# A hybrid attention and ConvFFN step on one core: a margin in the planner's TensorE list, a sample's loads traced later, and the sample's value product split by head

## The chip, the cores and the metric

One Trainium2 chip, one of its cores. The metric is the device time of one execution in microseconds (us); the median of several runs is compared. One further execution was recorded by the hardware profiler, and everything that is read below is read from that recording.

## The reference

One layer of a streaming encoder, run for a prompt of 1024 frames and a sample of 64 frames that share the weights, all in float32. The part that matters here:

```python
p = rms_norm(x, g_norm1) @ w_in            # q, k, v of 8 heads "A", 8 heads "B", forget logits
oa = softmax(qa ka^T / 8 + rel_bias) va    # A: band of 9 chunks of 64 frames
ob = softmax(qb kb^T / 8 + c_t - c_s) vb   # B: causal, c = running sum of log sigmoid(forget logits)
x += concat(oa, ob) @ w_o
x += mem_attend(rms_norm(x), mk, mv)       # 256 memory tokens; mk, mv = rms_norm(mem) @ w_mkv
x += conv_ffn(rms_norm(x))
```

The sample does the same with caches in front of its own keys and values: each of its 64 queries sees 512 cached rows (A) or 1024 cached rows (B) and then the sample's own 64. For each head the last step of its attention is a product of probabilities (64 queries by 576 or 1088 keys) with values (those keys by 64).

## The kernel before

TensorE products of float32 are made from two parts of each operand (`hi`, a float32r copy, and `lo`, the rest) in three products (`hi*hi`, `lo*hi`, `hi*lo`); only the sample's attention and a few small products use plain float32 operands.

The work goes in stages, heads in pairs. For each pair of heads the projection of eight blocks of 128 frames (L413, and L535 for the sample) is woven with the attention of blocks that are already projected: transposes of the normalised queries and keys (L484), a copy of the keys to the other half of the partitions by a DMA (L491, `k<-k`), scores (L706, into the one PSUM tile `S`), a reduction on VectorE that adds the bias and finds the extreme (L709, `mx`), the exponential on ScalarE (L711), the scaling on GpSimd (L713), transposes of the probabilities (L743, `PT<-ident,s`), their split into `pth` and `ptl` (L744 on ScalarE, L745 on VectorE), and the values (L762, `O`).

After the last pair comes the stage that most of the change touches. Its background work is the memory's keys and values, `mem @ w_mkv` (L829, `pj<-mw..`, in units of 128 by 256; `w_mkv` arrives by L813 as `mwraw` and is split by ScalarE at L821 and VectorE at L822). A finished unit of keys is scaled by VectorE (L958, `kv`) and turned by TensorE (L977). Into this the eight head pairs of the sample are woven, one `Sample` object for each in the order `SAMPLES`: `load` (L996 to L1005: queries, new values, cached keys and values), `load_bias` (L1014, L1016), `prep` (L1022), `score` (L1045 and L1046 on TensorE, L1048 and L1050 on VectorE, L1056 on ScalarE), `turn` (transposes L1069, copies to `pth` or `ptl` at L1071 and L1073), `sum` (the values, L1083) and `out` (L1093, L1095). A `sum` product takes the probabilities of both heads (128 columns, 64 for each head) as the stationary operand and the values of both heads (128 columns) as the moving one; of its 128 by 128 result only the two diagonal 64 by 64 blocks are used. There are 48 such products with 128 keys and 8 with the last 64 (`svn`). The output projection (L1183) follows, and its inputs are split at L1235 and L1236.

In the loop over the samples, step `x` weaves sample `x`'s scores, sample `x-1`'s turns and sums and sample `x+1`'s preparation with units of the background work. At the head of the step it loads the bias of sample `x+1` and the data of sample `x+3`.

What is traced up to the line that sets `arranged` (1627) is not executed in the order in which it was traced. `arrange` is a planner: it gives each instruction a cost, follows when each operand would be ready, and at every moment lets the engine that is free first take, of the instructions that are ready, the one that was traced earliest. The order that results is fixed on each engine (TensorE, VectorE, ScalarE, GpSimd, and the DMA queue of SyncE). All of it is in-order: an instruction whose operand is late holds up everything behind it on its engine. What is traced later than `arranged` keeps its traced order.

Of the kernel before, what the change touches and what calls it, by code (L numbers as in the profile page):

```python
# [9 lines left out]
ACT = mybir.ActivationFunctionType  # L10
# [7 lines left out]
S = 64  # L18
# [23 lines left out]
def hybrid_step(ctx: ExitStack, tc: tile.TileContext, i: dict, o: dict):  # L42
    nc = tc.nc
    act, dve, pool, pe = nc.scalar, nc.vector, nc.gpsimd, nc.tensor
# [343 lines left out]
    def weave(main, subs):  # L388
        j = 0
        for x, f in enumerate(main):  # L390
            f()
            while j * len(main) < len(subs) * (x + 1):
                subs[j]()
                j += 1
        for f in subs[j:]:
            f()
# [539 lines left out]
    kvs, stores, waiting = {}, [], []  # L936
# [45 lines left out]
    class Sample:  # L982
# [93 lines left out]
        def sum(self, c):  # L1076
            last = c == self.nc
            if c == 0:
                self.op = ps.tile([P, 2, P], F32, name="O", bufs=1)[:, 0]
            rows_, n = (S, 1) if last else (P, 4)  # L1080
            v = self.vraw.rearrange("p (o h) d -> p o h d", o=1) if last else self.v[c]
            for x in range(n):
                pe.matmul(self.op, self.pt[c][:rows_, x], v[:rows_, x].rearrange("p h d -> p (h d)"),  # L1083
                          start=c == 0 and x == 0, stop=last)
            if last:
                self.u = wk.tile([P, 64], F32, name="su", bufs=2)
                for h in range(2):
                    r = slice(h * S, h * S + S)
                    act.activation(self.u[r], self.op[r, h * S:h * S + S], ACT.Copy, scale=self.r[r])

        def out(self):
            tq = bank("PT").rearrange("p (a b) -> p a b", a=4)
# [37 lines left out]
    samples = [Sample(p) for p in SAMPLES]  # L1130
# [134 lines left out]
    for x in range(len(samples) + 1):  # L1265
# [4 lines left out]
        nxt = samples[x + 1] if x + 1 < len(samples) else None  # L1270
        if nxt:
            nxt.load_bias()
        if x + 3 < len(samples):
            samples[x + 3].load()
        if x in (5, 6):
            load_early(x - 5)
        new, fin = [], []
# [12 lines left out]
        elif ha:  # L1290
            main = pieces[4:] + [f for two in zip(split[1], first[1].pieces) for f in two]
            subs = [lambda: stream.upto(4)] + subs
        weave(main, subs)
        if cur:
            c = cur.nc
            old = [lambda z=z, u=cur: u.turn(z) for z in range(2)] + [lambda u=cur: u.sum(0)]
            old += ([lambda u=cur: u.turn(2), lambda u=cur: u.sum(1)] if c == 2 else [])
            old += [lambda u=cur, c=c: u.sum(c), cur.out]
# [243 lines left out]
    for n, u in enumerate(mems):  # L1542
        h, c = u.h, u.c
# [69 lines left out]
    for w, m in enumerate(ROWS):  # L1613
        x = long_row("qhi")
# [472 lines left out]
def arrange(tc, end):  # L2087

    import heapq

    signal = 0.07
    nodes, owner, made, touched, opened, closed = [], {}, {}, {}, {}, []
    writer, readers, group = {}, {}, {}
    setter = select = None
# [19 lines left out]
    def cost(ins, engine, kind, cols, rows, psum):  # L2114

        op = str(getattr(ins, "op", ""))
        if engine == "PE":
            if getattr(ins, "is_transpose", False):
                return 0.109, 0.35, False
            if ins.ins[0].bass_ap.dtype == F32:  # L2120
                o = max(0.214, cols * 0.00178)
            else:
                o = max(0.00087 * ins.ins[1].bass_ap.ap[1][1], 0.003 + cols * 0.000456)
            return o, o + 0.16, False
# [131 lines left out]
    while True:  # L2256
        start, engine = min((earliest(e), e) for e in ENGINES)
        if start == 1e9:
            break
        while coming[engine] and coming[engine][0][0] <= start:  # L2260
            n = heapq.heappop(coming[engine])[1]
            heapq.heappush(waiting[engine][nodes[n][6]], n)
        a, b = waiting[engine]
        line = min([x for x in (a, b if port <= start else []) if x], default=None)
        if line is None:
            continue
# [18 lines left out]
                    release(m)  # L2285
        for m, begun in after[n]:
            same = nodes[m][1] == engine
            ready[m] = max(ready[m], start + (0 if begun else busy if same and engine == "PE" else done if same and engine != "SP" else done + signal))
            missing[m] -= 1
            if not missing[m]:  # L2290
                release(m)
# [91 lines left out]
```

## Time and profile before

| | |
|---|---|
| time, median of 3 runs | 1693.71 us (1690.34, 1693.71, 1694.01) |
| the profiled execution, its own time | 1686.39 us |
| its span | 1684.6 us |
| TensorE busy | 1660.5 us, 99% of the span |
| VectorE, ScalarE, GpSimd busy | 1166.4, 907.9, 583.2 us |
| DMA, mean of the core's 16 DMA engines | 119 GB/s |

The span is the time from the first to the last recorded instruction; the execution's own time is 1.8 us more than that. The profiled execution is 7.3 us under the median of the three runs. TensorE (PE) records have modelled ends: a product counts as busy for some 0.2 to 0.4 us though the next one begins after about 0.12, so a wait shorter than that overlap does not appear as idle time of PE. It appears in the start times and in the waits of the weight loads (PEld).

### The profile page before, as it was taken

What the parts mean: (1) busy time and instruction counts of PE and PEld (TensorE: products, weight loads), DVE (VectorE), ACT (ScalarE), POOL (GpSimd) and SP (SyncE); (2) the same over time, 40 slices, a digit from 0 to 9 for tenths busy, and PEclk for the clock granted to TensorE, in tenths of its full rate; (3) what the DMA queues carried; (4) which work ended last, traced back from release to release, by engine and by line L of the source; (5) the groups of instructions that cost most, each with busy time, mean ns of one, the idle gap of its engine ahead of it and who ended that gap; (6) DMA issues with size and microseconds to landing.
All of it is one profiled execution on the core that took longest, in us unless ns stands there. A gap on an engine that the chain in (4) does not pass through costs nothing.

```text
span 1684.6 us, 33070 instructions
## 1 busy us (share of the span) xinstructions
PE 1660.5 (99%) x12027; PEld 1613.2 (96%) x12027; DVE 1166.4 (69%) x2584; ACT 907.9 (54%) x2003; POOL 583.2 (35%) x846
## 2 busy tenths in 40 slices
PE   9999999999999999999999999999999999999999
PEld 8899899999998879999999999999999999999999
DVE  7866866766778644344553797777777777559996
ACT  8866677767777564345555554333333333444442
POOL 1756688888853213444446111000000000000000
PEclk9999999999999999999999999999999999999999
DMA  7323243232235974421115632222222222983332
GB/s 242 91 77 84 76 113 91 77 92 84 64 118 165 290 216 152 141 82 58 55 58 162 214 115 84 77 78 77 78 77 77 78 78 84 320 298 120 102 109 88
DMA packets 142260, 199.82 MB, mean 119 GB/s; under 512 B 22200, under 2 KB 85304, under 8 KB 142096
## 3 DMA queue, kind: packets, MB, share of 16 engines
q1 hardware_dynamic: 142096, 197.70, 37.8%
q8 instruction: 95, 1.56, 0.4%
q14 instruction: 69, 0.57, 0.1%
HBM read 148.01 MB, written 43.34 MB: 114 GB/s over the span
## 4 chain that ended last, share of the span: by engine, by line
PE 87%; ACT 4%; DVE 4%; DMA 2%; issue 1%; SPq 0%; POOL 0%; DVEq 0%; ACTq 0%; POOLq 0%
PE W L1739 27%; PE W L2063 14%; PE pj L1183 14%; PE pj L413 11%; PE S L706 4%; PE O L762 3%; PE PT L743 3%; PE pj L829 2%; PE W L1183 1%; PE pj L535 1%; PE S L1475 1%; PE tq L1514 1%; PE O L1514 1%; PE tq L484 1%; DMA k<-k 1%
## 5 line engine op out<-in xcount | busy, mean ns | idle before, releaser
L413 PE MATMUL pj<-whi,xhi 128*128 128x384 f32 (+1 forms) x480 | 172.7, 360 | 0.0
L413 PE MATMUL pj<-whi,xlo 128*128 128x384 f32 (+1 forms) x480 | 164.7, 343 | 0.0
L413 PE MATMUL pj<-wlo,xhi 128*128 128x384 f32 (+1 forms) x480 | 164.1, 342 | 0.0
L1739 PE MATMUL W<-h,hi 128*128 128x272 f32 x704 | 134.3, 288 | 1.4 <-ACT qlo L1875 1.4
L1845 POOL COPY s<-gp 128x2 f32<-128x2 f32 x22 | 15.8, 719 | 336.1 <-DVE gp L1844 336.1
L2063 PE MATMUL W<-f,hi 128*128 128x272 f32 x672 | 127.2, 287 | 0.0
L745 DVE TENSOR_TENSOR ptl<-PT,pth 128x512 fp32r<-128x512 f32 (+2 forms) x192 | 97.9, 521 | 32.4 <-ACT pth L744 30.6
L713 POOL TENSOR_SCALAR s<-s,ssum 128x640 f32<-128x640 f32 (+7 forms) x128 | 92.9, 728 | 68.2 <-DVE ssum L712 52.2
L711 ACT ACTIVATE s<-s,mx 128x640 f32<-128x640 f32 (+7 forms) x128 | 94.5, 738 | 35.9 <-DVE mx L709 35.0
L744 ACT CAST pth<-PT 128x512 fp32r<-128x512 f32 (+2 forms) x192 | 84.6, 451 | 54.1 <-PE PT L743 52.4
L1739 PEld LDWEIGHTS W<-h,hi 128*128 128x128 f32 x704 | 110.3, 188 | 1.7 <-ACT qlo L1875 1.6
L2063 PEld LDWEIGHTS W<-f,hi 128*128 128x128 f32 x672 | 105.2, 188 | 0.1
L1739 PE MATMUL W<-h,lo 128*128 128x272 f32 x352 | 101.3, 288 | 0.0
L706 PE MATMUL S<-k,q 128*128 128x256 f32 (+3 forms) x432 | 90.5, 323 | 7.2 <-DVE mx L709 2.8
L2063 PE MATMUL W<-f,lo 128*128 128x272 f32 x336 | 96.7, 288 | 0.0
L1602 ACT CAST hi<-raw 128x512 fp32r<-128x512 f32 x68 | 42.2, 621 | 98.7 <-PE W L1739 59.2
L413 PEld LDWEIGHTS pj<-whi,xhi 128*128 128x128 f32 x480 | 90.6, 189 | 1.5
L413 PEld LDWEIGHTS pj<-wlo,xhi 128*128 128x128 f32 x480 | 90.8, 189 | 0.7
L413 PEld LDWEIGHTS pj<-whi,xlo 128*128 128x128 f32 x480 | 90.3, 188 | 0.4
L743 PE MATMUL PT<-ident,s 128*128 128x128 f32 x528 | 87.6, 273 | 0.8 <-DVE ptl L745 0.8
L706 PEld LDWEIGHTS S<-k,q 128*128 128x128 f32 x432 | 67.3, 188 | 21.8 <-DVE q L495 8.1
L1183 PE MATMUL pj<-a,hi 128*128 128x384 f32 (+1 forms) x352 | 87.2, 332 | 1.0 <-DVE a L1236 0.9
(611 smaller groups left out, 5684.3 us busy)
## 6 DMA issues: line engine op xcount, KB each, us to landing
raw<-in_w_down_dram SPq DMA_DIRECT2D x45, 256.0 KB, 2.7
wraw<-in_w_dram SPq DMA_DIRECT2D x56, 192.0 KB, 2.7
raw<-in_w_up_dram SPq DMA_DIRECT2D x41, 256.0 KB, 2.7
h<-ad SPq DMA_DIRECT2D x32, 272.0 KB, 5.1
mwraw<-in_w_mkv_dram SPq DMA_DIRECT2D x16, 512.0 KB, 5.6
raw<-in_w_mo_dram SPq DMA_DIRECT2D x32, 256.0 KB, 3.2
kvraw<-in_w_down_dram SPq DMA_DIRECT2D x32, 256.0 KB, 3.4
k<-k SPq DMA_DIRECT2D x60, 128.0 KB, 2.4
```

The costliest lines, as they stand in the source:

```text
L413: pe.matmul(pj[:, :nw], x_part(a, k, t * P, P), wt[k][b][:, :nw], start=n == 0, stop=n == 3 * KT - 1)
L706: pe.matmul(sp[:, a:a + m], q, ring[:, h, z, k0:k0 + m], start=z == 0, stop=z == 1)
L711: act.activation(s[:, :n], s[:, :n], ACT.Exp, bias=mx, scale=-1.0, accum_out=sm)
L713: pool.tensor_scalar(s[:, :n], s[:, :n], sm, 1.0, op0=ALU.mult, op1=ALU.mult)
L743: pe.transpose(pt[:, b - ch[0]], self.s[j][:, (b - w0) * P:(b - w0 + 1) * P], ident)
L744: act.copy(hi[:, f:f + n, j], pt[:, f:f + n])
L745: dve.tensor_tensor(lo[:, f:f + n, j], pt[:, f:f + n], f32(hi[:, f:f + n, j]), op=ALU.subtract)
L762: pe.matmul(op[:r, cols], v[:, :r], self.pts[b][m][:, x, cols], start=first and (b, m) == steps[0], stop=ch[-1] == self.last and (b, m) == ...
L1183: pe.matmul(out()[:, :cn], w[a][:, k % 4], x[b][k][:, c0:c0 + cn], start=k == 0 and (a, b) == SPLIT[0], stop=k == KT - 1 and (a, b) == SPL ...
L1602: act.copy(hi, t)
L1739: pe.matmul(w[:, z, :Q], a(p, j), rights[j][b][:, z * Q:z * Q + Q], start=fresh and begin and j == 0 and x == 0, stop=final and end and j ...
L2063: pe.matmul(ws[m][:, z, :Q], la[p][:, m * P:(m + 1) * P], ra[b][:, z * Q:z * Q + Q], start=first and y == 0 and what in opening, stop=fina ...
```

## The change

Four edits.

1. `sum` makes two products for each group of keys, one for each head: 64 columns of probabilities as the stationary operand, 64 columns of values as the moving one, into the partitions of that head. The two blocks that nobody used are not computed. The scaled copy to `su` becomes one instruction on 128 partitions in place of two on 64.
2. The planner's cost of a float32 product whose stationary operand has at most 64 columns is 0.077 us (it was at least 0.214).
3. `samples[x + 3].load()` is traced after the step's weave and not at its head, so that in the planner the step's other loads go before it.
4. A margin for TensorE, `sure["PE"] = 0.2`: while TensorE has anything else that is ready, an instruction joins its list only when its operands have been ready for 0.2 us by the planner's reckoning. Successors on TensorE itself are exempted by the same 0.2.

```diff
             for x in range(n):
-                pe.matmul(self.op, self.pt[c][:rows_, x], v[:rows_, x].rearrange("p h d -> p (h d)"),
-                          start=c == 0 and x == 0, stop=last)
+                for h in range(2):
+                    r = slice(h * S, h * S + S)
+                    pe.matmul(self.op[r, :64], self.pt[c][:rows_, x, r], v[:rows_, x, h], start=c == 0 and x == 0, stop=last)
             if last:
                 self.u = wk.tile([P, 64], F32, name="su", bufs=2)
-                for h in range(2):
-                    r = slice(h * S, h * S + S)
-                    act.activation(self.u[r], self.op[r, h * S:h * S + S], ACT.Copy, scale=self.r[r])
+                act.activation(self.u, self.op[:, :64], ACT.Copy, scale=self.r)
...
-        if x + 3 < len(samples):
-            samples[x + 3].load()
         if x in (5, 6):
             load_early(x - 5)
...
         weave(main, subs)
+        if x + 3 < len(samples):
+            samples[x + 3].load()
...
-    signal = 0.07
+    signal, sure = 0.07, {"PE": 0.2}
...
-                o = max(0.214, cols * 0.00178)
+                o = 0.077 if ins.ins[1].bass_ap.ap[1][1] <= 64 else max(0.214, cols * 0.00178)
...
-        while coming[engine] and coming[engine][0][0] <= start:
+        a, b = waiting[engine]
+        while coming[engine] and coming[engine][0][0] <= start - (sure.get(engine, 0.0) if a or b else 0.0):
             n = heapq.heappop(coming[engine])[1]
             heapq.heappush(waiting[engine][nodes[n][6]], n)
-        a, b = waiting[engine]
...
-            ready[m] = max(ready[m], start + (0 if begun else busy if same and engine == "PE" else done if same and engine != "SP" else done + signal))
+            ready[m] = max(ready[m], start + (0 if begun else busy - sure[engine] if same and engine == "PE" else done if same and engine != "SP" else done + signal))
```

The new order differs from the old one in many places on every engine, up to the output projection. Three places are shown here. The names are those of the sections above; a number behind a name is the buffer's.

First, TensorE at the end of the first pair of heads, where `S` is written for one tile of scores after another. Before:

```order
L706 MATMUL S_967<-k_416,q_841 128x384 x2
L706 MATMUL S_967<-k_416,q_841 128x256 x2
L706 MATMUL S_1030<-k_416,q_841 128x384 x2
L706 MATMUL S_1030<-k_416,q_841 128x256 x2
L535 MATMUL pj_929<-whi_178,xs_898 128x392
```

And after, with the sixteen products of L535 (the sample's projection) standing between the two tiles:

```order
L706 MATMUL S_967<-k_416,q_841 128x384 x2
L706 MATMUL S_967<-k_416,q_841 128x256 x2
L535 MATMUL pj_929<-whi_178,xs_898 128x392
...
L413 MATMUL pj_1021<-whi_779,xhi_182 128x384
L706 MATMUL S_1030<-k_416,q_841 128x384
```

The second tile's scores, which can begin only when VectorE has read the first tile out of `S`, moved behind the sample's projection.

Second, VectorE at the first sample's scores. `mr` is the reciprocal root that `kv` (L958) needs, and the ISA rows of L1048 are the reduction of the sample's 1024 scores. Before:

```order
L80 SCALAR_TENSOR_TENSOR mr<-rsq_a,rsq_y 128x1
L1048 ISA s,smx<-S,s 128x1024
L1048 ISA smx 128x1
L958 SCALAR_TENSOR_TENSOR kv<-pj,mr,gmk 128x256
L78 TENSOR_TENSOR rsq_a<-mms,rsq_y 128x1
```

And after:

```order
L80 SCALAR_TENSOR_TENSOR mr<-rsq_a,rsq_y 128x1
L958 SCALAR_TENSOR_TENSOR kv<-pj,mr,gmk 128x256
L1050 ISA s,smx<-tq,s 128x64
L1050 ISA smx 128x1
L78 TENSOR_TENSOR rsq_a<-mms,rsq_y 128x1
L1048 ISA s,smx<-S,s 128x1024
L1048 ISA smx 128x1
```

The scaled keys `kv`, for which TensorE's L977 waits, moved ahead of the long reduction.

Third, the DMA queue of SyncE, at the two loads of the last 256 columns of `w_mkv` (`mwraw_9181` and `mwraw_9198` before, `mwraw_9188` and `mwraw_9205` after). Before:

```order
L965 DMA vmd_8177<-kv_9063 128x256
L1014 DMA s_9142<-rows_75 64x576 x2
L996 DMA sqd_9145<-sqk_73 64x256
L998 DMA svn_9147<-sv_74 64x128
L1001 DMA kraw_9149<-in_cak_dram 64x512 x2
L1005 DMA vraw_9152<-in_cav_dram 128x512
L813 DMA mwraw_9181<-in_w_mkv_dram 128x1024
```

And after:

```order
L965 DMA vmd_8177<-kv_9062 128x256
L996 DMA sqd_9149<-sqk_73 64x256
L998 DMA svn_9151<-sv_74 64x128
L1001 DMA kraw_9153<-in_cak_dram 64x512 x2
L1005 DMA vraw_9156<-in_cav_dram 128x512
L1014 DMA s_9158<-rows_75 64x576 x2
L813 DMA mwraw_9188<-in_w_mkv_dram 128x1024
```

These read alike, but the group of loads ahead of `mwraw` is that of the seventh sample before (the third with `cak` in the queue) and that of the sixth after (the second with `cak`): of all loads one sample's fewer stands ahead.

## The prediction

> **What bounds the kernel now.** I read the page's busy times first, then the table by stage, then the waits of TensorE (PE), and then each long wait in the timeline.
>
> ```profile
> PE 1660.5 (99%) x12027; PEld 1613.2 (96%) x12027; DVE 1166.4 (69%) x2584; ACT 907.9 (54%) x2003; POOL 583.2 (35%) x846
> ```
>
> PE is busy for 1660.5 of 1684.6 us, so 24.1 us of idle time is all that a better order can give back, beside shorter products. The stretches of 50 us (columns: length; busy time and instructions of PE, PEld, DVE, ACT, POOL; granted clock; DMA share; GB/s) say where it is:
>
> ```profile
> 150.00:200.00 50.00, 48.32 (x311) 44.09 (x310) 38.88 (x106) 32.49 (x87) 30.00 (x42) 1.00 0.27 70
> 500.00:550.00 50.00, 47.13 (x356) 44.76 (x355) 39.66 (x110) 36.13 (x98) 20.98 (x33) 1.00 0.61 179
> 550.00:600.00 50.00, 46.57 (x331) 40.82 (x330) 29.62 (x82) 28.56 (x76) 8.51 (x16) 0.97 0.91 266
> 600.00:650.00 50.00, 48.02 (x310) 42.81 (x309) 25.66 (x69) 32.57 (x90) 10.18 (x9) 1.00 0.67 207
> 1100.00:1150.00 50.00, 50.00 (x402) 50.00 (x401) 39.58 (x68) 20.29 (x30) 3.28 (x9) 1.00 0.21 71
> ```
>
> The stretch at 1100 us, beyond the planner's part, has no idle time. The three from 500 to 650 us, with the sample's attention, lose 2.9, 3.4 and 2.0 us, 8.3 together, and one of them ran at a mean clock of 0.97. What PE waited for, whole run (us in total, times, longest):
>
> ```profile
> PE S L706 <- DVE mx L709: 2.8, 6, 1.0
> PE S L706 <- DMA k<-k: 2.6, 3, 2.1
> PE PT L977 <- DVE kv L958: 1.7, 1, 1.7
> PE O L1083 <- ACT pth L1073: 1.5, 1, 1.5
> PE pj L1183 <- DVE a L1236: 0.9, 1, 0.9
> ```
>
> They are few and each has a place. Under about 0.15 us a wait does not show here, because the record of the product before still counts as busy.
>
> **The value products.** Their price and that of their nearest kin:
>
> ```profile
> 553.37 0.33 PE L1046 MATMUL tq<-skn,sq 128*128 128x64 f32 x2
> 563.42 1.05 PE L1083 MATMUL O<-vraw,pth 128*128 128x128 f32 x8
> 566.72 0.28 PE L829 MATMUL pj<-mwlo,mhi 128*128 128x256 f32 x1
> 566.84 0.28 PE L829 MATMUL pj<-mwhi,mlo 128*128 128x256 f32 x1
> 567.04 0.49 PE L1083 MATMUL O<-svn,pth 64*128 64x128 f32 x2
> 567.37 0.28 PE L1022 MATMUL tq<-ident,sqd 64*128 64x64 f32 x2
> 87.38 0.34 PE L762 MATMUL O<-pth,v 128*128 128x256 f32 x2
> 87.56 0.23 PE L762 MATMUL O<-ptl,v 128*64 128x128 f32 x1
> 87.61 0.39 PE L413 MATMUL pj<-wlo,xhi 128*128 128x384 f32 x1
> L1083 PE MATMUL O<-vraw,pth x64: 271/275/377, 563.4 to 630.5; 128*128 128x128 f32 x64
> ```
>
> A plain float32 product leaves two records. Eight records of L1083 fill 1.05 us and one lasts 0.275, so they begin (1.05 - 0.275) / 7 = 0.11 us apart: 0.22 us for one product, for 48 products with 128 keys. L1046 has 64 moving columns; with the same 0.275 for its last record it shows 0.33 - 0.275 = 0.055 between the two, half of it. So a pair of 64-column products costs 4 x 0.055 = 0.22 us if they go in turn, which saves nothing, and 0.11 us if the two heads, which use different columns of the array, run beside each other. No row decides between them. I take 0.16, near the middle, where the diff's own 0.077 for one product (0.154 for two) also lies: 48 x 0.06 = 2.9 us saved (bounds 0 and 5.3). The 64-key product costs 567.37 - 567.04 = 0.33 us now. Its pair can cost 0.22 (8 x 0.11 = 0.9 us saved) or 0.66 (2.6 us lost); I take 0.44, since the second product's two records at 0.055 add 0.11, a loss of 0.9 us. Net: 2.0 us saved, bounds 6.2 saved and 2.6 lost.
>
> The row against this is that same one. It begins 0.20 us after the L829 ahead of it, where two L829 in a row begin 0.12 apart, and its two records are 0.49 - 0.275 = 0.21 apart and not 0.11: a product on half of the array's rows paid extra. On half of its columns the trace has the row at 87.56 (128*64), and there nothing is paid: the next product begins 0.05 us later. [...]
>
> **The wait of L977 at 553.7 us.**
>
> ```profile
> 553.35 0.15 DVE L80 SCALAR_TENSOR_TENSOR mr<-rsq_a,rsq_y 128x1 f32<-128x1 f32 x1
> 553.66 1.23 DVE L1048 CUSTOM_DVE_ANT_0 s<-S,s 128x1024 f32<-128x1024 f32 x1 [0.17 <-issue]
> 554.81 0.48 DVE L958 SCALAR_TENSOR_TENSOR kv<-pj,mr,gmk 128x256 f32<-128x256 f32 x1
> 555.44 0.41 PE L977 MATMUL PT<-ident,kv 128*128 128x128 f32 x2 [1.74 <-DVE kv L958]
> ```
>
> `mr` is ready at 553.50, but VectorE's queue has the sample's reduction ahead of `kv`. In the new order `kv` follows `mr`, and PE has one more L1045 product ahead of L977. `kv` would end near 554.0 and PE would come near 554.3: all of the 1.7 us goes (bounds 0.5, if the reduction's wait moves to another row, and 1.9).
>
> **The wait of the values at 588.8 us.** It is the DMA queue's doing:
>
> ```profile
> 579.47 1.69 SPq L1014 DMA_DIRECT2D s<-rows  x2
> 581.22 0.59 SPq L996 DMA_DIRECT2D sqd<-sqk  x1
> 583.91 0.84 SPq L1005 DMA_DIRECT2D vraw<-in_cav_dram  x1
> 584.85 0.38 SPq L813 DMA_DIRECT2D mwraw<-in_w_mkv_dram  x1
> 589.38 0.62 ACT L821 CAST mwhi<-mwraw 128x512 fp32r<-128x512 f32 x1 [3.29 <-DMA mwraw<-in_w_mkv_dram]
> 590.28 0.24 ACT L1073 COPY pth<-PT 64x128 f32<-64x128 f32 x1
> 590.57 0.48 PE L1083 MATMUL O<-svn,pth 64*128 64x128 f32 x2 [1.52 <-ACT pth L1073]
> 592.20:595.60 3.40, 3.40 (x15) 3.13 (x15) 1.39 (x3) 2.20 (x8) 0.00 (x0) 0.51 0.50 133
> ```
>
> ScalarE stood for 3.29 us before the split of `w_mkv`, with the copy that PE needed queued behind it. One sample's loads took the queue from 581.22 to 584.75, 3.5 us, just ahead of this `mwraw`. In the new order the queue has one such group fewer ahead of it, so it is issued up to 3.5 us earlier, more than the 3.29. I take the whole 1.5 us (bounds 0 and 1.6). The sample loads that now go later cannot be late: the seventh's, at 581 before, would go near 592, and its predecessors' rows are some 9 us apart with a lead of three steps. The last row (the granted clock is the number behind POOL's) shows PE at half clock for 3.4 us right after that wait, which cost 1.7 us; it is the only such stretch inside the span. If the wait goes I expect the dip to go. [...] I count 1.7 us, bounds 0 and 1.7.
>
> **The keys' copy at 526 us.**
>
> ```profile
> k<-k SPq DMA_DIRECT2D x60, 128.0 KB, 2.4
> DMA to landing us min/median/max: 6.1/6.1/6.1
> ```
>
> The copy that lands in 2.4 us by the median took 6.1 here, behind two `mwraw` of 512 KB, and the scores waited 2.1 us. The order of the queue is the same after. But the 384-column part of these scores now stands behind twelve instructions more (seven of L829 at 0.12, three of L762, two transposes, some 1.3 us in all), the split of `w_mkv` no longer stands between the two key copies on ScalarE (0.6 us), and on the other side the first part comes 0.9 us sooner after its transposes. 1.3 + 0.6 - 0.9 is 1.0, which I take (bounds -0.5 and 2.1).
>
> **The scores, and the end of the stage.**
>
> ```profile
> 56.58 0.74 PE L706 MATMUL S<-k,q 128*128 128x384 f32 x4
> 58.36 0.87 PE L706 MATMUL S<-k,q 128*128 128x384 f32 x4 [1.03 <-DVE mx L709]
> 60.04 0.42 PE L535 MATMUL pj<-whi,xs 128*128 128x392 f32 x1 [0.81 <-DVE ms L179]
> 623.55 0.29 ACT L1089 ACTIVATE su<-O,ssum 64x64 f32<-64x64 f32 x1
> 624.27 0.31 ACT L1089 ACTIVATE su<-O,ssum 64x64 f32<-64x64 f32 x1
> ```
>
> At 58.4 us the second tile waits for VectorE to empty `S`; sixteen L535 now stand between. L535 itself waits for the split of the sample's input (DVE again), so of 1.03 + 0.81 one wait of about 0.6 stays: 1.2 us saved. The other waits of L706 on `mx` (1.8 us in five, each with one or two products more in front of it now) and the hidden ones I put at 2 us saved (bounds 0 and 5). Against that, near 176 and 183 us two tiles of scores follow the work that they wait for with 1.4 and 0.8 us less of PE's work in between: 1.5 us lost (bounds 0 and 4). The L1236 wait at 623 us is behind a full ScalarE, which loses one of two `su` copies per sample: 0.5 us saved (bounds 0 and 1.2). Later loads and more instructions on PE's queue I price at nothing: the first have three steps of cover, and 56 instructions more are inside the products' price.
>
> **Sum.** 2.0 + 1.7 + 1.5 + 1.7 + 1.0 + 1.2 + 2.0 + 0.5 - 1.5 = 10.1 us. The profiled execution would go from 1686.4 to 1676.3; the median, which lies 7.3 us above it, from 1693.7 to 1683.6. I forecast 1684 us.
>
> **Rivals.** (a) *The products run in turn and the waits only move.* PE's list is refilled as tightly as before, so a late operand holds up the next instruction in place of the last. Then only L977 (1.7) and one of the others survive, less 1.5 for new waits: 1692 us, no change. For it: the waits on `mx` were up to 1.0 us and the margin is 0.2. Against: the three long ones have causes in other queues that the new order takes away. (b) *Only part comes.* The sample's waits go and the products give nothing, or the reverse: 1688 us. (c) *Slower: a product on half of the columns pays what the one on half of the rows pays.* At the 0.33 us of the `svn` row, 112 products cost 37 us in place of 48 x 0.22 + 8 x 0.33 = 13, 24 us more: 1694 + 24 - 8 = 1710. It decides from (13 + 8 + 3.4) / 112 = 0.22 us for one product. For it speaks the `svn` row, against it the row at 87.56; nothing shows the upper half of the columns.
>
> **Numbers.** Chances: the forecast (1677 to 1687) 0.53, (b) 0.22, (a) 0.17, (c) 0.08. No change means within 0.2% (3.4 us), about what repeated runs can tell: the three shown differ by 3.7 us. So faster 0.75, same 0.17, slower 0.08. The range from 1676 to 1692 leaves out (c) and the ends of the bounds.
>
> **What would show it.** The value products of one chunk (sixteen records): 0.45 to 0.9 us, of which 0.64 is my value. No wait of L977 at the first sample; ScalarE without a wait for `mwraw` over 1 us; no stretch at half clock after the first 10 us; PE idle between 500 and 650 us down from 8.3 to about 4; L706 on `mx` under 1.5 us in total. Records of the values 0.2 us apart, or new waits of L706 over 3 us, would make me wrong.

## The result and the profile after

The changed kernel takes 1680.3 us (median of 6 runs, 1678.4 to 1685.4), the kernel before 1693.5 (6 runs on the same chip, 1689.0 to 1695.2): the ratio is 0.9932, with a 95% interval of 0.9913 to 0.9951. The forecast was 1684. The profiled execution went from 1686.4 to 1678.4, its span from 1684.6 to 1676.6. So the profile shows 8.0 us and the medians 13; that gap of 5 us is itself one of the findings below.

In the lines of after, the sum of the values is L1085 (before L1083); L1182, L1235 and L1738 were L1183, L1236 and L1739. Busy time, the stretches of the sample's stage and the longest waits of PE, with the columns of the prediction's:

```profile
PE 1654.5 (99%) x12139; PEld 1609.8 (96%) x12139; DVE 1161.7 (69%) x2584; ACT 905.3 (54%) x1995; POOL 583.1 (35%) x846
```

```profile
500.00:550.00 50.00, 48.62 (x369) 45.50 (x369) 40.05 (x113) 36.60 (x98) 18.48 (x33) 1.00 0.69 202
550.00:600.00 50.00, 46.70 (x434) 38.56 (x432) 28.03 (x77) 27.63 (x72) 5.37 (x9) 1.00 0.77 230
600.00:650.00 50.00, 47.17 (x313) 41.61 (x314) 26.01 (x63) 28.96 (x77) 13.73 (x11) 1.00 0.72 224
```

```profile
PE PT L743 <- DVE ptl L745: 1.8, 4, 0.6
PE PT L977 <- DVE kv L958: 1.6, 1, 1.6
PE O L1085 <- ACT pth L1073: 1.4, 2, 1.0
PE pj L1182 <- DVE a L1235: 1.4, 2, 0.9
...
PE S L706 <- DVE mx L709: 1.2, 3, 0.7
PE O L762 <- DVE mix L771: 1.1, 1, 1.1
PE S L706 <- DMA k<-k: 1.1, 2, 0.9
```

Busy time fell by 6.0 us, and idle time in the span only from 24.1 to 22.1. Between 500 and 650 us, where most of the forecast's idle time was to go, PE idles for 7.5 us in place of 8.3; the list of waits has lost the long ones of L706 and has grown at L743 (0.8 us before) and L762 (0.4). The half clock is gone: the granted clock is 1.00 in each of these stretches.

Most of what was won in attention does not show as idle time. Near 520 us of before, where both kernels have done the same 3326 products, the changed one is 5.5 us ahead, and its idle time up to there is only 1.7 us less (9.1 for 10.9). The rest left the busy time; I take it for waits that were hidden there, since the record of a product still counts as busy while the next one waits (an L829 for 0.28 us, where the next can begin after 0.12). The scores won of both kinds. The groups of L706 (busy time, mean ns, idle time ahead of it with what ended it), first of before and then of after:

```profile
L706 PE MATMUL S<-k,q 128*128 128x256 f32 (+3 forms) x432 | 90.5, 323 | 7.2 <-DVE mx L709 2.8 <-DMA k<-k 2.6 <-DVE q L495 0.9
```

```profile
L706 PE MATMUL S<-k,q 128*128 128x256 f32 (+3 forms) x432 | 91.6, 320 | 3.3 <-DVE mx L709 1.2 <-DMA k<-k 1.1 <-DVE q L495 0.3
```

Idle time ahead of the scores fell by 3.9 us. Counted from each score's start to the next record's start, hidden waits included, the 432 records took 74.9 us before and 69.7 after, 5.2 less.

The value products of one chunk between two L829, with the instructions on both sides (timeline of PE, first in before and then in after, where an `svn` pair stands below):

```profile
584.73 0.28 PE L829 MATMUL pj<-mwhi,mlo 128*128 128x256 f32 x1
584.85 1.05 PE L1083 MATMUL O<-vraw,pth 128*128 128x128 f32 x8
585.66 0.36 PE L829 MATMUL pj<-mwhi,mhi 128*128 128x256 f32 x1
585.86 0.28 PE L829 MATMUL pj<-mwlo,mhi 128*128 128x256 f32 x1
```

```profile
577.87 0.28 PE L829 MATMUL pj<-mwhi,mlo 128*128 128x256 f32 x1
578.08 0.69 PE L1085 MATMUL O<-vraw,pth 128*64 128x64 f32 x16
578.69 0.39 PE L829 MATMUL pj<-mwhi,mhi 128*128 128x256 f32 x1
578.91 0.28 PE L829 MATMUL pj<-mwlo,mhi 128*128 128x256 f32 x1
...
560.80 0.33 PE L1085 MATMUL O<-svn,pth 64*64 64x64 f32 x4
561.06 0.33 PE L1022 MATMUL tq<-ident,sqd 64*128 64x64 f32 x2
```

Sixteen records take 578.69 - 578.08 = 0.61 us up to the next instruction, so a pair costs 0.153, and the eight of before took 0.81. But the sixteen begin 0.21 us after the L829 ahead of them, 0.09 later than an L829 would, and the second L829 behind them comes a little later too. From the L829 ahead to the second one behind, the chunk takes 1.04 us in place of 1.13. The svn pair takes 0.26.

Two waits of the prediction's list, as they stand now (rows of ScalarE, VectorE and PE in the timeline of after):

```profile
547.28 0.38 PE L977 MATMUL PT<-ident,kv 128*128 128x128 f32 x2
548.88 0.62 ACT L821 CAST mwhi<-mwraw 128x512 fp32r<-128x512 f32 x1 [2.39 <-DMA mwraw<-in_w_mkv_dram]
549.41 0.20 ACT L77 ACTIVATE rsq_y<-rsq_y 128x1 f32<-128x1 f32 x1
549.72 1.22 DVE L1048 CUSTOM_DVE_ANT_0 s<-S,s 128x1024 f32<-128x1024 f32 x1
552.06 0.48 DVE L958 SCALAR_TENSOR_TENSOR kv<-pj,mr,gmk 128x256 f32<-128x256 f32 x1
552.68 0.41 PE L977 MATMUL PT<-ident,kv 128*128 128x128 f32 x2 [1.57 <-DVE kv L958]
...
581.77 0.62 ACT L821 CAST mwhi<-mwraw 128x512 fp32r<-128x512 f32 x1 [2.58 <-DMA mwraw<-in_w_mkv_dram]
582.96 0.33 PE L1085 MATMUL O<-svn,pth 64*64 64x64 f32 x4 [0.95 <-ACT pth L1073]
```

The L977 that waited before, the fifth of the eight units of keys, no longer does: its `kv` follows `mr` (546.17 and 546.56 us), and it starts at 547.28 without a wait. The 1.57 us belong to the sixth unit, whose L977 (at 558.28 in before) did not wait. Its `mr` is late for two reasons. The root's second step on ScalarE (L77) stands behind a split of `w_mkv` that waited 2.39 us, and VectorE's queue now has the sample's reduction (L1048, 1.22 us) between that step and `mr`. The values wait 0.95 us in place of 1.52, with the same mechanism.

### The profile page after: what moved, and what is told of

The parts are those of the page before. It is cut to its first block, busy times and chain, and to the rows that moved or that the text cites. A ratio compares the mean times of both kernels' runs of the same rounds, so it can differ in the third digit from the quotient of the medians.

```text
span 1676.6 us, 33258 instructions
## 1 busy us (share of the span) xinstructions
PE 1654.5 (99%) x12139; PEld 1609.8 (96%) x12139; DVE 1161.7 (69%) x2584; ACT 905.3 (54%) x1995; POOL 583.1 (35%) x846
## 4 chain that ended last, share of the span: by engine, by line
PE 87%; DMA 4%; DVE 4%; ACT 3%; issue 1%; SPq 1%; POOL 0%; DVEq 0%; ACTq 0%; POOLq 0%
PE W L1738 27%; PE pj L1182 14%; PE W L2062 14%; PE pj L413 11%; PE S L706 4%; PE O L762 3%; PE PT L743 3%; PE W L1182 2%; PE pj L829 2%; PE pj L535 1%; PE S L1474 1%; DMA wraw<-in_w_dram 1%; PE tq L1513 1%; PE O L1513 1%; DMA mwraw<-in_w_mkv_dram 1%
## 5 line engine op out<-in xcount | busy, mean ns | idle before, releaser
L1738 PE MATMUL W<-h,hi 128*128 128x272 f32 x704 | 134.3, 288 | 1.4 <-ACT qlo L1874 1.4
L1738 PEld LDWEIGHTS W<-h,hi 128*128 128x128 f32 x704 | 110.3, 188 | 1.7 <-ACT qlo L1874 1.6
L1738 PE MATMUL W<-h,lo 128*128 128x272 f32 x352 | 101.3, 288 | 0.0
L743 PE MATMUL PT<-ident,s 128*128 128x128 f32 x528 | 95.6, 274 | 3.0 <-DVE ptl L745 1.8
L706 PE MATMUL S<-k,q 128*128 128x256 f32 (+3 forms) x432 | 91.6, 320 | 3.3 <-DVE mx L709 1.2
L1182 PE MATMUL pj<-a,hi 128*128 128x384 f32 (+1 forms) x352 | 82.9, 331 | 1.4 <-DVE a L1235 1.4
L706 PEld LDWEIGHTS S<-k,q 128*128 128x128 f32 x432 | 69.9, 188 | 12.0 <-DVE q L495 3.6
```

The source lines that it names most:

```text
L706: pe.matmul(sp[:, a:a + m], q, ring[:, h, z, k0:k0 + m], start=z == 0, stop=z == 1)
L743: pe.transpose(pt[:, b - ch[0]], self.s[j][:, (b - w0) * P:(b - w0 + 1) * P], ident)
L1182: pe.matmul(out()[:, :cn], w[a][:, k % 4], x[b][k][:, c0:c0 + cn], start=k == 0 and (a, b) == SPLIT[0], stop=k == KT - 1 and (a, b) == SPL ...
L1738: pe.matmul(w[:, z, :Q], a(p, j), rights[j][b][:, z * Q:z * Q + Q], start=fresh and begin and j == 0 and x == 0, stop=final and end and j ...
```

## The experiments

The table sums up all runs. "Half clock" is the time at half clock inside the span, without its first 10 and last 2 us; for a stretch of 3.41 us I count half of that, 1.7 us, an estimate from the granted clock of 0.50. (The rows of before show 1.5: L829 begin 0.21 us apart between 592.46 and 593.32 us, and 0.12 apart outside the stretch.) The last three columns are one profiled execution less the first one of before: at the first and at the last L829 (519.9 and 617.3 us there: shortly before the end of attention, and almost the end of the sample's stage), and in the span.

| kernel | ratio to before, 95% interval | half clock, us | first L829 | last L829 | span |
|---|---|---|---|---|---|
| before | | 3.4 | 0 | 0 | 1684.6 |
| before, second profile (e11) | | 10.2 | +2.0 | +4.4 | +5.2 |
| before, third profile (e12) | | 6.8 | -0.1 | +5.6 | +6.2 |
| after | 0.9932 (0.9913 to 0.9951) | 0 | -6.4 | -9.0 | -8.0 |
| e1 products alone | 0.9995 (0.9983 to 1.0006) | 10.2 | -1.1 | +3.1 | +4.0 |
| e2 later loads alone | 0.9982 (0.9971 to 0.9993) | 6.8 | +2.1 | +2.2 | +3.4 |
| e3 margin alone | 0.9949 (0.9933 to 0.9965) | 3.4 | -7.6 | -8.7 | -7.7 |
| e4 after without later loads | 0.9966 (0.9953 to 0.9978) | 6.8 | -6.9 | -3.8 | +0.3 |
| e5 after, heads in turn | 0.9949 (0.9933 to 0.9965) | 0 | -6.6 | -7.8 | -4.5 |
| e6 margin and later loads | 0.9931 (0.9917 to 0.9946) | 3.4 | -6.1 | -6.0 | -6.5 |
| e7 after, exact comparison | 0.9934 (0.9918 to 0.9949) | 3.4 | -7.4 | -8.1 | -7.2 |
| e8 exact, values together | 0.9916 (0.9902 to 0.9930) | 6.8 | -4.1 | -6.1 | -6.1 |
| e9 after, values together | 0.9940 (0.9927 to 0.9952) | 3.4 | -6.5 | -6.6 | -7.8 |
| e10 e9 with a margin of 0.4 | 0.9950 (0.9936 to 0.9965) | 10.2 | -11.5 | -9.7 | -10.0 |

Median times stand on different chips, where before took 1693.5 (after), 1690.2 (e1 to e4), 1692.5 (e5 to e8) and 1688.6 (e9, e10); compare ratios. The column of the first L829 flatters the kernels with the margin: seven instructions of attention (thirteen in e10) that stood ahead of it in before stand behind it there. At equal work near 520 us the difference is 0.9 us smaller (1.5 in e10): 5.5 us in after, 6.7 in e3, 10.0 in e10.

**The parts alone.** Four kernels carry the change's edits apart. e1 has the products, with the single `su` copy (the lines that go are those of the change):

```
+                for h in range(2):
+                    r = slice(h * S, h * S + S)
+                    pe.matmul(self.op[r, :64], self.pt[c][:rows_, x, r], v[:rows_, x, h], ...)
+                o = 0.077 if ins.ins[1].bass_ap.ap[1][1] <= 64 else max(0.214, cols * 0.00178)
```

> The kernel before with only the value products by heads, their planned duration of 0.077 us and the single su copy; the planner's margin and the place of the loads stay. Theory (the two heads run beside each other, a drain of about 0.09 us on entry and exit): 12 groups of 16 records at 0.70 us with their entry in place of 0.89, 8 svn pairs at 0.26 in place of 0.33: 2.3 + 0.6 = 2.9 us less, some 1 us of it given back where the last sample's products stand apart: 2 us faster, 1691.5 when the kernel before takes 1693.5. Rival A (the products are worth nothing by themselves, only the order moved): within 1 us of before. Rival B (a lone product's drain outweighs): 1 to 3 us slower. The waits of L977 at 553.7 and of the values near 589 stay in all of these.

Measured 0.9995: 0.8 us, with an interval from 2.9 faster to 1.0 slower: inside rival A's 1 us, with the theory's 2 us not excluded. The records themselves are as in after (0.69 us for sixteen). The stage around them lost more in this execution, because the wait of the values was not 1.5 us but 4.15, behind a split on ScalarE that waited 4.82 us for `mwraw` (PE in the timeline, then the stretch after it):

```profile
593.64 0.48 PE L1085 MATMUL O<-svn,pth 64*64 64x64 f32 x4 [4.15 <-ACT pth L1073]
```

```profile
592.95:599.78 6.83, 6.13 (x26) 5.18 (x27) 3.05 (x5) 3.90 (x12) 0.00 (x0) 0.50 0.45 131
```

Here TensorE runs nothing in the 3.41 us ahead of the stretch (589.54 to 592.95 us), and 6.83 us at half clock follow.

e2 has the later loads:

```
-        if x + 3 < len(samples):
-            samples[x + 3].load()
...
         weave(main, subs)
+        if x + 3 < len(samples):
+            samples[x + 3].load()
```

> The kernel before with only the sample's loads traced one step's work later. Theory (the loads of 581 to 585 us held up a w_mkv transfer, and through ScalarE's queue the values): the wait of 1.5 us near 588.8 and the half-clock stretch behind it (1.7 us) go: 3 us faster, 1690.5 when before takes 1693.5; ScalarE waits less than 1 us for mwraw there. Rival A (the transfer is late for its own reasons, 512 KB each in a full queue): no wait goes, within 1 us. Rival B (it takes the margin to use the free slot): 0 to 1 us faster, the mwraw wait gone and another in its place.

Measured 0.9982, 3.0 us faster (1.2 to 4.9): the theory's size. Its profile has the wait gone and the half clock with it (the weight load of the same product):

```profile
594.30 0.29 PEld L1083 LDWEIGHTS O<-svn,pth 64*128 64x128 f32 x2 [0.27 <-ACT pth L1073]
```

ScalarE's wait for `mwraw` did not fall under 1 us, as I had expected: it is 1.83 there, with the copy no longer so long behind it. And the half clock turned up, at 60.03 and 531.07 us, behind two other waits, those of the scores at 58 and of the key copy at 526 us, which stand in before as well but cost only themselves in its first profile. So this span is longer than before's, where the times say faster.

e3 has the margin:

```
+    signal, sure = 0.07, {"PE": 0.2}
...
+        while coming[engine] and coming[engine][0][0] <= start - (sure.get(engine, 0.0) if a or b else 0.0):
...
+            ready[m] = max(ready[m], start + (0 if begun else busy - sure[engine] if same and engine == "PE" ...
```

> The kernel before with only the margin of 0.2 us for TensorE in the planner's list. Theory (the margin carries what the change won before 512 us, where there is no value product and no sample's load): 6 us less at the first step of the memory's products, and in all 5 to 7 us faster, 1687.5 when before takes 1693.5; the wait of L706 on k<-k near 526 us is 1 us or less. Rival A (the margin only trades waits; what came before 512 us is also the other two edits' doing, by the planner's order): 0 to 2 us faster. Rival B (worth even more without the lone products at the end): 9 to 11 us faster, as much as the whole change.

Measured 0.9949, 8.6 us faster (5.9 to 11.3), between the theory and rival B, and 6.7 us stand already near 520 us in the profile (equal work), near the theory's 6; rival A falls. The miss is the key copy, for which the waits still show 1.7 us.

e4 is the changed kernel with the loads back at their old place.

> The changed kernel with the sample's loads traced where they were before. Theory (the loads alone cure the wait for mwraw at 585 to 589 us): ScalarE waits over 2 us for one mwraw there, the values wait over 1 us and the half-clock stretch may follow: 1.5 to 3.5 us slower than the changed kernel, near 1683 when before takes 1693.5. Rival A (the margin had already cured it): within 1 us of the changed kernel, 1680.5. Rival B (loads at the old place serve the sample better): 1 to 2 us faster than the changed kernel.

Measured 0.9966 against 0.9932, 5.7 us slower than the changed kernel; by the two intervals together 2 to 10. Its profile shows the mechanism in a row, on DMA queue, ScalarE and PE, and the stretch after it:

```profile
578.88 0.58 SPq L1005 DMA_DIRECT2D vraw<-in_cav_dram  x1
...
579.57 0.38 SPq L813 DMA_DIRECT2D mwraw<-in_w_mkv_dram  x1
...
585.23 0.62 ACT L821 CAST mwhi<-mwraw 128x512 fp32r<-128x512 f32 x1 [5.16 <-DMA mwraw<-in_w_mkv_dram]
...
586.42 0.48 PE L1085 MATMUL O<-svn,pth 64*64 64x64 f32 x4 [3.84 <-ACT pth L1073]
```

```profile
586.41:593.24 6.83, 6.82 (x27) 5.51 (x28) 2.44 (x5) 3.20 (x9) 0.00 (x0) 0.50 0.54 150
```

The sample's `vraw` goes out just ahead of the `mwraw` that ScalarE stands for; 3.84 us of waiting in place of 0.95, and 3.4 us counted for 6.83 us at half clock, are 6.3 us; at the last L829 this kernel is 5.2 us behind the changed one, so other places won back the rest; beyond it this execution loses another 3.1 us, where TensorE's order is the same in both. The 5.7 us are more than the theory's 1.5 to 3.5, which took the wait from before's first profile, but the interval reaches down to 2. What all profiles show together is stronger than this pair. With the loads at their old place (before three times, e1, e3, e4) the transfer went out 0.5 to 1.6 us before ScalarE was free for its split, and the values waited 1.1 to 4.2 us, 2.8 on average. With the later loads (after, e2 and e5 to e9) it went out 1.7 to 4.0 us before, and they waited 0 to 1.8 us, 0.7 on average.

e6 is the kernel before with margin and loads (the diffs of e2 and e3 together), without the products.

> The kernel before with the margin and the later loads, without the products by heads. Theory (margin 8.6 and loads 3.0 us add up; the products' 1.5 us are given back at the end of the stage, where they stand one by one): the time of the changed kernel within 1 us, 11.6 us faster than before. Rival A (the products are worth their 1.5 to 2 us in the whole): that much slower than the changed kernel. Rival B (the lone products cost more than the rest of them brings): 1 to 2 us faster than the changed kernel.

Measured 0.9931, the changed kernel's 0.9932: the theory. The products by heads add nothing that can be measured (between 4 us more and 4 less, by the two intervals).

**Why the products add nothing.** e5 issues the heads one after the other:

```
-            for x in range(n):
-                for h in range(2):
+            for h in range(2):
+                for x in range(n):
```

> The changed kernel, but a chunk's four products of the first head are issued before the four of the second, where the change issues the two heads by turns. The planner gives the order of instructions otherwise as it was. Theory (the two heads, on different columns of the array, run beside each other only because they are issued by turns): records of one head 0.055 us apart, a chunk's sixteen in 0.88 us in place of 0.615, 12 x 0.27 = 3.2 us slower than the changed kernel. Rival (a 64-column product simply costs 0.077 us in any order): still 0.6 us a chunk, the time of the changed kernel within 1 us.

```profile
558.15 0.97 PE L1085 MATMUL O<-vraw,pth 128*64 128x64 f32 x16
```

The same sixteen records now fill 0.97 us (0.69 in after): 0.28 for each of eleven chunks and 0.12 for the last, 3.2 us by the rows. The span is 3.5 us longer than after's, both without half clock; that it fits so well is chance, since this execution misses after's waits between 582 and 587 us (2.1 us) and loses 2.2 us beyond 614 us, most of it near 930 and 980 us. The ratio 0.9949 against 0.9932 has about the rows' size (2.9 us, though the two intervals together, 4 us either way, do not exclude 0). So the two heads do run beside each other when they are issued by turns; a 64-column product alone costs 0.11 us, as the prediction's upper price had it. In the trace the records of the two heads begin 6 ns apart, and the pairs follow at 0.058 us.

What took the gain back stands at the end of the stage. The last sample's products do not come in one group there (PE in the timeline of after):

```profile
618.85 0.44 PE L1182 MATMUL pj<-a,hi 128*128 128x384 f32 x1
619.22 0.33 PE L1085 MATMUL O<-vraw,pth 128*64 128x64 f32 x2
619.48 0.79 PE L1182 MATMUL pj<-a,hi 128*128 128x384 f32 x3
```

A lone product lasts 0.26 us, and it begins 0.37 after an L1182 in a row whose members are 0.17 apart: 0.46 us in all, in place of the 0.077 that the planner reckons with. The reason is in the margin's comparison. The next product of a sum becomes ready at start + busy - 0.2 and is compared with start - 0.2 of the next round; the two should be equal, and the rounding of floats decides. Where it comes out late, another ready product goes between. Three kernels test that; in e1, without the margin, the last chunk stands apart too (2, 2 and 12 records), so the margin is not the only cause. e7 only adds 1e-6:

```
-... <= start - (sure.get(engine, 0.0) if a or b else 0.0):
+... <= start - (sure.get(engine, 0.0) if a or b else 0.0) + 1e-6:
```

> The changed kernel with 1e-6 added in the margin's comparison. By it the next product of a sum, ready exactly at the margin in the planner's reckoning, is no longer held back by the rounding of a float, and sums stand together again. Theory: the last sample's eight lone products stand in four groups: 1.5 us faster than the changed kernel, if attention keeps its gain. Rival (the alternation of two sums, which the rounding makes, is part of what attention won, since it puts more work between an operand and its use): 2 to 5 us slower than the changed kernel, lost before 512 us.

e8 also prefers a value product after a value product, and e9 does that while 1e-6 counts only there, so that attention keeps after's order:

```
+        last = order[engine][-1] if engine == "PE" and order[engine] else None
+        pairs = last is not None and nodes[last][4] == 0.077
-... <= start - (sure.get(engine, 0.0) if a or b else 0.0):
+... <= start - (sure.get(engine, 0.0) if a or b else 0.0) + 1e-6 * pairs:
-        n = heapq.heappop(line)
+        n = min([m for m in line if pairs and nodes[m][4] == 0.077] or line)
```

> The same 1e-6, and after one value product the planner's list takes the next value product first, if it is ready, so that a chunk's eight stand together everywhere. Theory: the 3 us given back at the end of the stage are kept: 2 to 3 us faster than the changed kernel, 1.5 faster than with the 1e-6 alone. Rival (as for the 1e-6 alone: attention loses): 1 to 3 us slower than the changed kernel, but still 1 to 2 us faster than with the 1e-6 alone.

> The changed kernel, with the comparison as it is except that, after a value product, the list takes the next value product first if it is ready (the 1e-6 counts only there). Attention's order is that of the changed kernel to the word, and each chunk's eight products stand together. Theory: the 3 us that the lone products gave back at the end of the stage are kept and nothing else moves: 2 to 3 us faster than the changed kernel, a ratio near 0.9915 to before. Rival: the lone products filled places where TensorE would have waited (for the memory's mixing input): within 1 us of the changed kernel.

The last sample's sixteen records stand in groups of 6, 2, 2, 2, 2 and 2 in after and of 6, 2, 2 and 6 in e7, which differs by the 1e-6 alone, so a difference of that size does decide there. In e8 and e9 they stand together (PE in the timeline of e9):

```profile
620.82 0.69 PE L1085 MATMUL O<-vraw,pth 128*64 128x64 f32 x16 [0.48 <-ACT pth L1073]
```

The same 23 products, from 618.85 us in after and from 621.04 in e9, take 4.76 us there and 2.53 here: grouping is worth 2.2 us. That is shown by the traces. The times do not show it: 0.9934, 0.9916 and 0.9940 against 0.9932 are all within their intervals of the changed kernel. e8 has the best ratio of the study and the lowest median (1677.2 us), but no kernel here is shown to beat the changed one. The trace of e9 says what covers a gain of 2 us. Its orders on TensorE and on the DMA queue are those of after up to the first sample's svn pair near 560 us, and yet (PE in the timeline, and the stretch after it):

```profile
523.76 0.62 PE L706 MATMUL S<-k,q 128*128 128x384 f32 x2 [2.43 <-DMA k<-k]
```

```profile
524.41:527.82 3.41, 3.41 (x18) 3.41 (x17) 2.31 (x9) 1.30 (x3) 0.78 (x1) 0.50 0.67 177
```

The same key copy, at the same place of the same queue, landed in 5.6 us in after and in 7.1 here. The wait is 2.43 us in place of 0.91, and a half-clock stretch follows that after did not have: with 1.7 counted for it, 3.2 us between two executions of one order. The rival of e7 (attention needs the alternation) is not decided either: its first L829 stands at -7.4, no worse than after's -6.4, while e8's stands at -4.1, with one half-clock stretch near 61 us.

**The size of the margin.** e10 is e9 with `{"PE": 0.4}`.

> The same with a margin of 0.4 us in place of 0.2. Theory (the waits that the margin takes away are errors of the planner's durations, most of them under 0.2 us, since each hidden wait was too short to show): no better than 0.2, 0 to 2 us slower, because a longer margin holds back work that was ready. Rival (the visible waits that stay, 0.4 to 1.6 us, are errors larger than 0.2): 2 to 4 us faster than with 0.2.

Measured 0.9950, no better than 0.2, as the theory said, though its reason is not shown: attention gained more (10.0 us at equal work in place of e9's 5.6), and the sample's stage lost it, in a stretch of three windows at half clock that begins after a wait of L977 for 1.83 us:

```profile
543.48 0.41 PE L977 MATMUL PT<-ident,kv 128*128 128x128 f32 x2 [1.83 <-DVE kv L958]
```

```profile
544.80:555.04 10.24, 7.09 (x24) 4.95 (x23) 6.02 (x20) 5.05 (x14) 2.84 (x10) 0.50 1.06 348
```

**Why the medians moved by more than the profile.** The kernel before, unchanged, was profiled twice more.

> The kernel before, once more under the profile. Theory (after a window of 3.41 us in which TensorE idled for 1.2 us or more, the next window may run at half clock and lose 1.7 us; whether a wait falls into one window is chance, so that a kernel with many waits over 1 us pays for a varying number of them): half-clock stretches of 3.41 us or twice that at one or more of the waits near 58, 526, 553 and 589 us, not the same as in the first profile, and a span of 1682.9 us plus 1.7 for each 3.41, within 1.5. Rival (the half clock belongs to a fixed place in the kernel): one stretch, near 592 us, as in the first.

> The kernel before a third time, with the same two expectations: by the theory the number and places of the half-clock stretches differ again between the three profiles, and the spans differ by 1.7 us for each; by the rival all three have the one near 592 us.

The half-clock stretches of the second profile, then of the third, and between them the longest wait of the third:

```profile
60.32:63.73 3.41, 3.41 (x12) 3.41 (x11) 2.99 (x9) 2.89 (x10) 3.39 (x4) 0.50 0.18 59
531.36:534.77 3.41, 3.41 (x19) 3.41 (x18) 2.41 (x10) 1.90 (x6) 0.21 (x1) 0.50 0.61 147
596.21:599.62 3.41, 3.41 (x17) 3.06 (x17) 1.59 (x4) 2.63 (x9) 0.00 (x0) 0.50 0.52 154
```

```profile
PE O L1083 <- ACT pth L1073: 4.0, 1, 4.0
```

```profile
529.19:532.60 3.41, 3.41 (x18) 3.41 (x18) 2.31 (x10) 1.70 (x6) 0.01 (x1) 0.50 0.57 151
597.45:600.87 3.42, 3.42 (x18) 3.05 (x17) 1.62 (x4) 2.63 (x9) 0.00 (x0) 0.50 0.54 155
```

One, three and two stretches in three executions of one kernel, at the waits of the scores (58 us), the key copy (526) and the values (589 to 594): the theory on their number and places holds, and the rival falls. The spans, 1689.8 and 1690.8, are longer than 1682.9 + 1.7 for each (1688.0 and 1686.3) by 1.8 and 4.5 us, outside the 1.5 that I had given: the waits differ as well. The values waited 1.52, 1.91 and 3.96 us in the three, each time for a `mwraw` transfer. So the first profile of before was a favourable one. The mean of the three spans is 1688.4, after's is 1676.6: 11.8 us, which is near the 13 of the medians and the 11.5 that the ratio gives. After has one profile only, of the fastest of its six executions.

## Why the prediction was right, and where not

The time came out 3.7 us below 1684, inside the likeliest case's 1677 to 1687. The sum of 10.1 us met a change of 8.0 in the profile and of 13 in the medians. That it came so near is in part luck: its terms erred both ways, and what carried the change, the scores, I had at 1.7 of the 10.1. Of the signs that I gave, the sixteen records (0.69 us), the half clock and L706 on `mx` (1.2 us) came as said; the waits for `mwraw` under 1 us and the idle time of about 4 us did not, and L977 still waits, at another unit.

- *Products, 2.0 us.* The pair costs 0.153 us, where I took 0.16, and the svn pair 0.26, where I took 0.44 on the strength of a row whose two records are themselves 0.21 apart. But the records are not the whole price: entry and exit take back more than half of the 0.2 us that a chunk's records save, which leaves 0.08 to 0.09. An svn pair between two L829 is 0.16 us shorter (0.69 for 0.85 us with both L829 counted, 570.46 to 571.15 in after and 577.21 to 578.06 in before), and no shorter where L1022 follows. By these rows I estimate some 2 us for the twelve chunks and eight pairs where each chunk stays together. That is the size of my term, by luck: I had 2.9 for the chunks and a loss of 0.9 for the pairs. In after the lone products give back 2.2 of it, which the sum did not have: I had read that the last groups of products were there, and not how they stood in the order. Net nothing, which is what e6 says.
- *Entry and exit.* I had put the row at 87.56, where nothing is paid, above the `svn` row. For these products the runs show both: the two heads work at the same time (a chunk's records fill 0.69 us by turns and 0.97 in e5, where they do not), and going in and out costs 0.09 us each way. In after the sixteen records at 578.08 begin 0.21 us behind the L829 ahead, where two L829 stand 0.12 apart, and the L829 behind them begins 0.15 us after the last pair, where the pairs follow at 0.058. What e1's expectation calls a drain is this time; no run shows what TensorE does in it. Not every instruction on half of the columns pays it: the transpose of `su` at 586.11 us in after (L1092, 128*64) is followed by an L829 0.06 us later, as the row at 87.56 was. What decides that is open.
- *Rival (c)*, a price of 0.33 us for every 64-column product, is refuted for products in a group, but a price above that exists: a lone product cost 0.46.
- *L977, 1.7 us.* 0.2 came. The step itself held: "`mr` is ready at 553.50, but VectorE's queue has the sample's reduction ahead", and with the reduction moved, that L977 waits no longer. The low bound failed, "0.5, if the reduction's wait moves to another row": it moved into the chain of the next unit's `mr`, where ScalarE's wait for `mwraw` (2.39 us) had already made the root late, and L977 waits 1.57 us there. I did not ask what is late next on the engines that feed the waiter. This is rival (a) in one place.
- *Values and half clock, 1.5 + 1.7 us.* 0.6 and 1.7 in the profile (the 1.7 by the granted clock; by the rows of L829 it was 1.5), more in the times: 3.0 us for the loads alone (e2), 5.7 within the whole (e4). The mechanism, loads ahead of a `mwraw` in the queue, is what the profiles show together; the size hung on an execution in which the wait was short. One step was too large: "it is issued up to 3.5 us earlier". Against the moment when ScalarE is free for the split, the transfer goes out only 0.45 us earlier in after than in before's first profile (1.69 us ahead in place of 1.24), because one sample's group still stands just ahead of it.
- *Key copy, 1.0 us.* 1.2 in after, but e9 with the same order waits 2.43 us, as long as before did (2.12, 1.81, 1.89). Two things set this wait. From the issue of the first copy to the moment when PE has run out of other work it is 4.0 us in all five profiles of the old order (before three times, e1, e2) and 5.4 us in all eight with the margin of 0.2. So the instructions that I counted are there, and cover 1.3 us more. The other is the transfer: from issue to the scores it took 5.9 to 6.3 us in the five and 5.8 to 7.8 in the eight. On average the wait fell from 2.05 to 1.4 us.
- *Scores.* For the place at 58 us I had 1.2. At equal work the gain grows from 0.1 us at 57.0 us to 2.0 at 63.5, so both waits went (1.03 and 0.81), though by 93 us it is down to 0.9 again. For the rest of attention I had 2.0 less 1.5; the gain is 5.5 us near 520 us, new waits at L743 and L762 included. So 5.5 came where I had 1.7. This is the term that was mis-sized, by 3.8 us, because I counted the waits on `mx` that the list shows and only guessed at the hidden ones. e3 puts the whole margin at 8.6 us: it carries the change.
- *The end of the stage, 0.5 us.* It did not come: PE waits for `a` (L1235) for 1.4 us in two places, where it was 0.9 in one.
- *The sample's stage.* Idle from 8.3 to "about 4" us: it is 7.5. L977's wait moved, and new waits of 0.5 us at the values, 0.7 at `su` and 0.5 at `a` took the place of those removed, which is rival (a) in this one stage.
- *The offset.* I carried the 7.3 us between before's profiled execution and its median over to the new kernel. It is 1.9 there. The step "the median, which lies 7.3 us above it" treated as constant what was the number and the length of waits that happened to be short in the one execution.

## What to carry to other kernels

A planner that trusts its own durations to the last nanosecond places an instruction where its operand is just ready, and every small error can become a wait; leaving 0.2 us between an operand and its use was worth 8.6 us here. Near 520 us 6.7 us of it stand in the profile of e3, and only 2.6 of these were idle time that a list of waits shows. Where one product is split in two that run beside each other, issue them by turns and keep them in one group: here a chunk took 0.97 us one head after the other in place of 0.69, and going in and out of these products cost TensorE 0.09 us each way. And before a gain of a few microseconds is read from two profiles, profile the kernel before more than once: waits on transfers, and the half clock behind them, differed by 6 us between executions of one program.

## What the runs showed of the hardware

In these profiles the granted clock fell to 0.50 for whole windows of 3.41 us, one, two or three of them (3.41 us in before, 6.83 in e1 and e4, 10.24 in e10), on a grid that does not start with the kernel. In the second profile of before the stretches begin at 60.32, 531.36 and 596.21 us, 138 and 19 windows apart to within 0.01 us; the first one of the third profile, at 529.19, is 137.4 windows from that 60.32. A window need not be empty: the windows ahead of the stretches had between 1.2 us (e3, at 616.7 us) and 3.4 us (e1, e4) of idle time, while one with 1.6 us in before (56.4 to 59.8) and one with 1.6 in after (549.5 to 552.9) had no stretch behind them. In all fourteen profiles together, without their first and last microseconds, each of the fourteen windows with 1.8 us of idle time or more had a stretch behind it; of those with less, four had one (1.17 us in e3, 1.52 in before, 1.64 and 1.75) and most had none, one of 1.74 among them. So in these runs idle time alone does not decide below 1.8 us, and what does is open.

A DMA wait is not a fixed number. The key copies of 128 KB landed in 5.6 us (after) or 7.1 (e9) in the same order, and the waits of the values behind `mwraw` were 1.5, 1.9 and 4.0 us in three executions of before; the wait of the scores on VectorE at 58 us was 1.03 us in all three.
